# A two-layer decoder on one core: the order of the experts, the place of the excess code and of the scaling of x

## The chip, the cores and the metric

The kernel runs on one core of a Trainium2 chip. The metric is the device time of one execution in microseconds (us). A core has the engines TensorE (PE for its matmuls, PEld for its weight loads), VectorE (DVE), ScalarE (ACT) and GpSimd (POOL); SyncE (SP) issues nearly all DMAs here. "MB" below is one weight tile of 128 x 2048 fp32.

## The reference

Two decoder layers over 256 tokens of width 1024. In each layer three mixers (a convolution, differential attention, a gated linear recurrence) run on x and are merged, then `x = LN(alpha*x + mix)`; then a mixture of 32 experts, and `x = LN(alpha*x + moe)`. This is the part that the change touches:

```
g_idx = argmax(t @ wg + bg)                      # one of 4 groups per token
top_v, top_i = top_k(elog of that group, 2)      # two of its 8 experts
comb[token, expert] = softmax(top_v) * p_group
for e in range(32):
    h = silu(t @ w1[e]) * (t @ w3[e])            # w1, w3: 1024 x 512
    out = out + comb[:, e] * (h @ w2[e])         # w2: 512 x 1024
x = layer_norm(alpha * x + out)
```

An expert has 6 tiles of 1 MB (two each of w1, w3 and w2), all read from HBM in fp32. How many of the 512 token-expert pairs fall to an expert is known only when the kernel runs.

## The kernel before, in words

**Order of the experts.** Experts 0 to 3 are fixed. The other 28 are sorted on the chip by their number of tokens, rank 0 being the fullest (`sort`, L925), and `GROUPS` (L27) says in which order the ranks are worked: each tuple is four blocks of 32 token slots. Ranks 0 to 6 may use three blocks, 7 to 14 two, the rest one (`width`, L32). "Expert e" below is the e-th in this order: with the old order ranks 2, 3, 4, 5, 6 are experts 17, 19, 21, 23, 25 and ranks 27, 26, 25 are experts 22, 24, 26; experts 30 and 31 are the last group. Each block of an expert stands in an `If` on its count (`blocks`, L1282): a block without tokens is jumped over, and SP also jumps over the loads of an expert without tokens (L1414, L1415).

**Weights.** SP loads tiles into four rings of buffers, A to D, taken in the fixed order of `RING_ORDER` (8 B, 5 C, 5 A, 3 D: 21 tiles, L51). `room()` (L990) takes the next buffer, whether it is then filled or not, so an expert without tokens takes six buffers that stay empty. A load waits until the tile 21 places earlier has been used. At the end of iteration e the loads up to group e+3 are issued; a group is w1 and w3 of its expert and w2 of the one before.

**An iteration e** on PE: `between(e)` (L1346: the scatter of the last full group into the four output banks `po`, L1206 and L1207, then `turn_g(e-1)`, L1343, which transposes the hidden values of expert e-1), `hidden(e)` (L1305), `project(e-1)` (L1329), and for every eighth block the gather of the next token list (L1066, then L1081 to L1096). ACT and DVE split each projection in two fp32r halves (`split_y`, L1314 and L1316). In iteration 30 `between` also adds x to the banks (L1355), which needs x scaled.

**Three pieces near the end of the loop.** In iteration 25 `spilled()` (L1254) takes six buffers and jumps, on PE, DVE, ACT and SP, over code for experts that have more tokens than their blocks hold (`extra`, L1218; the trace has no instruction of it). In iteration 26 the last token list is gathered, and after the loads of that iteration `rows_of(0)` (L995) loads gain and bias of the norm into one buffer with two DMAs, and `affine` (L336) lets POOL compute `x = (x*g + b)*ALPHA` in twelve instructions (L340, L341, L343). x is raw before that; `gather` applies gain and bias to the gathered rows (`affine_g`, L1050).

**The next layer's small work.** `cw` (L506, the convolution's weights halved) and `ch` (L568, the gates' bias halved) are one DVE instruction each, behind a DMA (L505, L567). The kernel is scheduled by a planner that orders each engine's queue by its own simulated times, so such an instruction can stand in a queue far ahead of its place in the code.

The end of a layer (after the loop) projects expert 31 (L1440), adds it to the banks (L1446), and normalises (L1448 to L1466). L1440 comes behind `turn_g(31)`, and that behind `project(30)`.

Of the kernel before, what the change touches and what calls it, by code (L numbers as in the profile page):

```python
# [16 lines left out]
OP = mybir.AluOpType  # L17
# [6 lines left out]
STATIC = 4  # L24


GROUPS = [(8, 9), (10, 11), (12, 13), (0, 15), (14, 16, 17), (1, 18), (2, 19), (3, 20), (4, 27), (5, 26), (6, 25),  # L27
          (7, 21, 22), (23, 24)]
ORDER = [r for g in GROUPS for r in g]


# [9 lines left out]
NB = 4 * (len(GROUPS) + STATIC // 2)  # L41
NS = NB - 2 * STATIC
OWNER = [e for e in range(NE) for _ in range(width(e))]
ALPHA = (2 * DEPTH) ** 0.25
EPS = 1e-5
KC = 31
# [26 lines left out]
C_W, C_B, C_LG, C_LB, C_N = 0, 124, 128, 132, 136  # L73
G_B, G_LN, G_N = 0, 24, 56
# [94 lines left out]
def kernel(ctx: ExitStack, tc: tile.TileContext, *aps, layers=DEPTH, experts=NE, dbg=None):  # L169
# [3 lines left out]
    V, S, T, G = nc.vector, nc.scalar, nc.tensor, nc.gpsimd  # L173
# [24 lines left out]
    x = cp.tile([128, 2, 1024], F32, name="x")  # L198
# [137 lines left out]
    def affine(dst, g, b, eng, scale=1.0):  # L336

        for tb in range(2):
            for c in (slice(0, 512), slice(512, 1024)):
                eng.tensor_mul(dst[:, tb, c], x[:, tb, c], g[:, 0, c])  # L340
                eng.tensor_add(dst[:, tb, c], dst[:, tb, c], b[:, 0, c])  # L341
                if scale != 1.0:
                    eng.tensor_scalar(dst[:, tb, c], dst[:, tb, c], scale, None, op0=OP.mult)  # L343
# [5 lines left out]
    for l in range(layers):  # L349
# [4 lines left out]
        ch = lc.tile([128, G_N], F32, name="ch")  # L354
# [148 lines left out]

        cw = wk.tile([128, C_N], F32, name="cw")
        nc.sync.dma_start(cw, A["conv"][l])  # L505
        V.tensor_scalar(cw[:, C_W:C_W + 4 * KC], cw[:, C_W:C_W + 4 * KC], 0.5, None, op0=OP.mult)  # L506
        u = wk.tile([128, 4, 286], F32, name="u")
        G.memset(u[:, :, 0:30], 0.0)
        yc = wk.tile([128, 4, 256], F32, name="yc")
        pa2 = chunk_cm(1)  # L510
        begun = S.activation(yc, pa2, AF.Tanh, scale=0.5)
        pa1 = chunk_cm(0)
        V.scalar_tensor_tensor(u[:, :, 30:286], yc, 1.0, pa1, op0=OP.add, op1=OP.mult)

        with tc.high_priority(offset=-CONV_LOW):
            for pair in range(2):
# [48 lines left out]
            split(lth[:, tb, :], ltl[:, tb, :], pt)  # L565
        pq = chunk_cm(5)
        nc.sync.dma_start(ch, A["chan"][l])  # L567
        V.tensor_scalar(ch[:, G_B:G_B + 24], ch[:, G_B:G_B + 24], 0.5, None, op0=OP.mult)  # L568
        masks = wk.tile([128, 256], F32, name="masks")
        nc.sync.dma_start(masks, A["c_f"][:, F_UP + 128:F_UP + 384])  # L570
        ones, negm = masks[:, 0:128], masks[:, 128:256]
# [64 lines left out]
        for part in (1, 0):  # L636
            E = []
            for tb in range(2):
# [3 lines left out]
                for h in range(4):  # L642
# [8 lines left out]
                    for o, mv in pieces:  # L651
                        n = mv.shape[1]
# [342 lines left out]
        def rows_of(which):  # L995

            gb = room().rearrange("p (i d) -> p i d", i=2)
            for i in range(2):
                nc.sync.dma_start(gb[:, i, :], rowbc(A["lnp"][l, 2 * which + i], 1024))
            return gb  # L1000
# [49 lines left out]
        def affine_g(dst, src, k):  # L1050

            g, b = ch[:, G_LN + k:G_LN + k + 1], ch[:, G_LN + 8 + k:G_LN + 9 + k]
            if k % 2:
                return S.activation(dst, src, AF.Identity, bias=b, scale=g)
            return V.tensor_scalar(dst, src, g, b, op0=OP.mult, op1=OP.add)

        def gather(xg, gt, n):

            step = 512 // n
            for d0 in range(0, 8, step):  # L1060
                tag = ("gt", "h", "h", "y")[d0 // step % 4]
                pg = PB(tag, [128, step, n], 1 + (tag == "h"))
                for d in range(step):
                    c = slice(128 * (d0 + d), 128 * (d0 + d) + 128)
                    for tb in range(2):
                        mm = T.matmul(pg[:, d, :], x[:, tb, c], gt[:, tb, :], start=tb == 0, stop=tb == 1)  # L1066
                done = [affine_g(xg[:, d0 + d, :], pg[:, d, :], d0 + d) for d in range(step)]
            return [i.ins for i in (mm, *done[-2:])]

        def slots(gt, tb, n=256):  # L1070
# [147 lines left out]
        def extra(W, code_of, comb_of, base):  # L1218

            g1 = ew.tile([128, 2, 64], F32, name="gt4", bufs=1)  # L1220
            for tb in range(2):
                V.tensor_scalar(g1[:, tb, :], slot, float(base), code_of(tb), op0=OP.add, op1=OP.is_equal)

            def T2(shape):
                return ew.tile(shape, F32, name="ov", bufs=1)

            xo = T2([128, 8, 64])
            gather(xo, g1, 64)
            w = ew.tile([64, 1], F32, name="wso", bufs=1)
            pw = PB("gt", [64, 1], 1)  # L1230
            for tb in range(2):
                T.matmul(pw, g1[:, tb, :], comb_of(tb), start=tb == 0, stop=tb == 1)
            S.copy(w, pw)
            ps = PB("h", [128, 512], 2)
            mm_hidden(ps[0:64], ps[64:128], lambda k: xo[:, k, :], W, range(8))
            g = T2([64, 512])
            swiglu(g, ps[0:64], ps[64:128], w)
            gt = ew.tile([128, 4, 64], F32, name="sto", bufs=1)
            transpose_g(gt, g)
            ps = PB("y", [128, 512], 1)  # L1240
            pa, pb = ps[0:64, :], ps[64:128, :]
            mm_out(pa, pb, gt, W)
            pt = PB("gt", [64, 2, 128], 1)
            for tb in range(2):
                T.transpose(pt[:, tb, :], g1[:, tb, :], ident)
            st = ew.tile([64, 2, 128], F32, name="sto", bufs=1)
            S.copy(st, pt)
            for half, src in enumerate((pa, pb)):
                y = T2([64, 512])
                S.copy(y, src)  # L1250
                for tb in range(2):
                    T.matmul(po[half][tb], st[:, tb, :], y, start=False, stop=False)
# [108 lines left out]
        for e in range(experts):  # L1361
# [18 lines left out]
                scatter(sts[NB // 4 - 2])  # L1380

            b0 = 8 * len(lists_of)
            if b0 < NB and (OWNER[b0] == e + 2 or b0 == NB - 4 and e == experts - 6):
                n = min(8, NB - b0) // 4
                gt = ew.tile([128, 2, 256], F32, name="gt4", bufs=1)
                for tb in range(2):
                    slots(gt, tb, 128 * n)
                xg_next = ew.tile([128, 8, 256], F32, name="xg")
                with ExitStack() as after:
                    for ins in gather(xg_next[:, :, 0:128 * n], gt[:, :, 0:128 * n], 128 * n):  # L1390
                        after.enter_context(tc.issue_after(ins))
                    end = next((i for i in range(OWNER[b0], experts) if FIRST[i] >= b0 + 8), experts)
                    tokens(OWNER[b0], end - OWNER[b0])
                ws_next = ew.tile([128, 2, 4], F32, name="ws")
                weigh(ws_next, gt, lambda tb, i: comb_s[:, tb, b0 - 8 + 4 * i:b0 - 4 + 4 * i], n)
                lists_of[b0 // 8] = xg_next, ws_next
                st = turn(gt, n)
                for i in range(n):
                    sts[b0 // 4 + i] = st[:, i]
            if e == experts - 7:  # L1400

                spilled()

# [3 lines left out]
            for d in dict.fromkeys(p[0] for p in pieces):  # L1407
# [7 lines left out]
                with tc.If(sizes_sp[d] > 0, preferred_fallthrough_block=True):  # L1415
                    n = nc.values_load(who[0:1, d:d + 1], min_val=0, max_val=NE - 1, engines=[ENG.SP])
                    for w in ws_:
                        fetch(*w, n)
            if e == experts - 6:

                gb = rows_of(0)
                affine(x, gb[:, 0:1], gb[:, 1:2], G, ALPHA)
        if l == layers - 1:
            gb = rows_of(1)
        st = sm.tile([128, 2, 2, 6], F32, name="lnst")
# [66 lines left out]
```

## Time and profile before

| | us |
|---|---|
| median of 3 runs | 1570.54 |
| the runs | 1568.11, 1570.54, 1581.56 |
| the profiled execution, its time | 1580.48 |
| its span, first to last instruction | 1578.7 |
| PE busy | 1305.4 (83%) |
| DVE busy | 754.8 (48%) |
| ACT busy | 540.1 (34%) |
| POOL busy | 309.2 (20%) |
| mean granted TensorE clock | 0.939 |

The profiled execution is 9.9 us above the median, and 1.8 us of its time lie outside its span. The page also cuts the span in 40 slices: the DMA engines are full (9 tenths and over 400 GB/s) in slices 10 to 20 and 29 to 39, which are the experts of the two layers, and half empty while the mixers run. A row of the timeline gives start, duration, engine, line, operation and tiles, and in brackets how long the engine sat idle before it and what ended that.

### The profile page before, as it was taken

Reading aid. Unit: us, or ns where it says so; the run is one execution under the profiler, and the core shown is the slowest. Engines: PE = TensorE matmul, PEld = TensorE weight load, DVE = VectorE, ACT = ScalarE, POOL = GpSimd, SP = SyncE. Lnnn points to the kernel's source line nnn. Section 1 sums busy time; section 2 is a strip of 40 time slices with the busy share of each in tenths; the row PEclk is TensorE's granted clock in tenths of the full one; section 3 lists DMA queues with packets and bytes.
Section 4 is the critical chain, followed back from the end, with each engine's and each line's share of the span. In section 5 each row is a group of like instructions: output and inputs, shape, how many; then the busy total and the mean of one; then the engine's idle time right before and its main releaser. Section 6 shows DMA issues by size and latency. Waiting matters only on the chain. (4 is left out here: it accounts for less than half of the span.)

```text
span 1578.7 us, 32663 instructions
## 1 busy us (share of the span) xinstructions
PE 1305.4 (83%) x12222; PEld 966.4 (61%) x12222; DVE 754.8 (48%) x1721; ACT 540.1 (34%) x1200; POOL 309.2 (20%) x247
## 2 busy tenths in 40 slices
PE   8999999897886877765688999989888877787664
PEld 8878999764553544442287889987555545454332
DVE  4999876732222222121258998767432232322114
ACT  5744655322221222111246445553222221222111
POOL 5644432200000000001265553412000000000012
PEclk9999999899999999988889999999899999999688
DMA  9433448969999999989944334568799999997694
GB/s 352 158 113 114 144 138 348 360 268 417 418 418 416 417 412 417 413 362 417 379 145 157 128 108 147 174 242 345 290 405 417 414 417 417 414 402 306 263 369 165
DMA packets 72791, 481.66 MB, mean 305 GB/s; under 512 B 8576, under 2 KB 9600, under 8 KB 17152
## 3 DMA queue, kind: packets, MB, share of 16 engines
q1 hardware_dynamic: 72288, 478.27, 77.0%
q8 instruction: 135, 2.21, 0.6%
q14 instruction: 80, 0.66, 0.1%
q10 hardware_dynamic: 288, 0.52, 0.1%
HBM read 477.71 MB, written 1.05 MB: 303 GB/s over the span
## 5 line engine op out<-in xcount | busy, mean ns | idle before, releaser
L422 POOL TENSOR_TENSOR wlo<-wa,whi 128x512 fp32r<-128x512 f32 x187 | 253.7, 1365 | 317.2 <-ACT whi L421 309.9
L421 ACT CAST whi<-wa 128x512 fp32r<-128x512 f32 x312 | 190.9, 620 | 192.0 <-PE mm L429 102.4
L1316 DVE TENSOR_TENSOR yl<-y,yh 32x256 fp32r<-32x256 f32 (+1 forms) x252 | 104.8, 416 | 245.8 <-ACT yh L1314 160.8
L430 PE MATMUL mm<-xh,wlo 128*128 128x256 f32 x640 | 184.9, 289 | 8.5 <-DVE wlo L422 7.3
L428 PE MATMUL mm<-xh,whi 128*128 128x256 f32 x640 | 184.4, 288 | 5.4 <-ACT whi L421 5.3
L429 PE MATMUL mm<-xl,whi 128*128 128x256 f32 x640 | 183.9, 287 | 0.0
L1154 DVE SCALAR_TENSOR_TENSOR g<-g,h 64x256 f32<-64x256 f32 x73 | 30.2, 413 | 319.8 <-ACT g L1153 267.3
L340 POOL TENSOR_TENSOR x<-x,wa 128x512 f32<-128x512 f32 x8 | 9.9, 1274 | 825.6 <-DMA wa<-in_lnp_dram 825.6
L1305 PE MATMUL h<-wb,xg 128*32 128x256 f32 x1888 | 144.0, 414 | 27.1 <-DMA wb<-in_w_dram 18.2
L1314 ACT CAST yh<-y 32x256 fp32r<-32x256 f32 (+1 forms) x252 | 90.8, 360 | 194.3 <-PE y L1329 190.1
L1153 ACT ACTIVATE g<-h 64x256 f32<-64x256 f32 x73 | 27.5, 377 | 377.4 <-PE h L1305 377.4
L430 PEld LDWEIGHTS mm<-xh,wlo 128*128 128x128 f32 x640 | 124.4, 194 | 10.7 <-DVE wlo L422 8.3
L428 PEld LDWEIGHTS mm<-xh,whi 128*128 128x128 f32 x640 | 124.9, 195 | 5.8 <-ACT whi L421 5.6
L422 DVE TENSOR_TENSOR wlo<-wa,whi 128x512 fp32r<-128x512 f32 x125 | 98.8, 797 | 58.0 <-ACT whi L421 58.0
L429 PEld LDWEIGHTS mm<-xl,whi 128*128 128x128 f32 x640 | 124.8, 195 | 1.0 <-issue 0.3
L1305 PEld LDWEIGHTS h<-wb,xg 128*32 128x32 f32 x1888 | 71.6, 117 | 86.2 <-DMA wb<-in_w_dram 28.5
L526 DVE SCALAR_TENSOR_TENSOR pc<-u,cw,pc 128x256 f32<-128x256 f32 x232 | 112.9, 487 | 4.1
L1305 PE MATMUL h<-wa,xg 128*32 128x256 f32 x1136 | 96.2, 416 | 9.2 <-PEq L1284 3.4
L429 PE MATMUL mm<-wlo,xh 128*128 128x512 f32 x208 | 84.6, 407 | 3.7 <-DVE wlo L422 3.7
L428 PE MATMUL mm<-whi,xh 128*128 128x512 f32 x208 | 83.2, 401 | 1.6 <-ACT A L615 1.6
L430 PE MATMUL mm<-whi,xl 128*128 128x512 f32 x208 | 83.2, 400 | 0.0
L1305 PE MATMUL h<-wc,xg 128*32 128x256 f32 x912 | 75.5, 388 | 6.5 <-DMA wc<-in_w_dram 3.1
(411 smaller groups left out, 2356.7 us busy)
## 6 DMA issues: line engine op xcount, KB each, us to landing
wb<-in_w_dram SPq DMA_DIRECT2D x137, 1024.0 KB, 10.5
wc<-in_w_dram SPq DMA_DIRECT2D x87, 1024.0 KB, 10.1
wa<-in_w_dram SPq DMA_DIRECT2D x83, 1024.0 KB, 9.9
wd<-in_w_dram SPq DMA_DIRECT2D x47, 1024.0 KB, 10.7
wa<-in_w_cm_dram SPq DMA_DIRECT2D x39, 1024.0 KB, 5.0
wa<-in_w_tm_dram SPq DMA_DIRECT2D x20, 1024.0 KB, 5.0
wa<-in_w_br_dram SPq DMA_DIRECT2D x12, 1024.0 KB, 5.0
wa<-in_w_out_dram SPq DMA_DIRECT2D x8, 1024.0 KB, 5.6
```

The lines of the kernel that those rows point to most:

```text
L340: eng.tensor_mul(dst[:, tb, c], x[:, tb, c], g[:, 0, c])
L421: S.copy(hi, wv)
L422: (V if npiece[0] > 4 * l and npiece[0] % 4 < share[0] else G).tensor_sub(lo, wv, hi)
L428: T.matmul(ps, ah, bh, start=first, stop=False)
L429: T.matmul(ps, ah, bl, start=False, stop=False)
L430: T.matmul(ps, al, bh, start=False, stop=last)
L526: V.scalar_tensor_tensor(yc[:, b, :] if j == KC - 1 else acc[:, i, :], u[:, b, j:j + 256], wv, acc[:, i, :], op0=OP.mult, op1=OP.add)
L1153: S.activation(g[:, c], p1_[:, c], AF.Tanh, scale=0.5)
L1154: V.scalar_tensor_tensor(g[:, c], g[:, c], 1.0, p1_[:, c], op0=OP.add, op1=OP.mult)
L1305: T.matmul(ps[32 * q:32 * q + 32, :], xg[:, k, 32 * j:32 * j + 32], W[q // 2][k // 4][:, f:f + 256], start=k == 0, stop=k == 7)
L1314: S.copy(yh[o:o + n, c], p)
L1316: V.tensor_sub(yl[o:o + n, c], p, yh[o:o + n, c])
```

## The change

Four edits: another order of the groups (the ranks 25, 26, 27 go from experts 26, 24, 22 to 29, 25, 21; ranks 2, 3, 4 from 17, 19, 21 to 20, 22, 24; the group of one-block experts from 27 to 29 goes to 17 to 19); the last gather from iteration 26 to 27, `rows_of(0)` from the end of iteration 26 to 25 ahead of that iteration's loads, `affine` from 26 to 27; `spilled()` from 25 to 28, with its gather taking x already scaled (one DVE instruction instead of eight on DVE and ACT); and L506 and L568 made to issue after the DVE instruction that writes `u`, in their own layer.

```diff
-GROUPS = [(8, 9), (10, 11), (12, 13), (0, 15), (14, 16, 17), (1, 18), (2, 19), (3, 20), (4, 27), (5, 26), (6, 25),
-          (7, 21, 22), (23, 24)]
+GROUPS = [(8, 9), (10, 11), (12, 13), (0, 15), (14, 16, 17), (1, 18), (7, 21, 22), (2, 27), (3, 19), (4, 26), (5, 20),
+          (6, 25), (23, 24)]
...
-        V.tensor_scalar(cw[:, C_W:C_W + 4 * KC], cw[:, C_W:C_W + 4 * KC], 0.5, None, op0=OP.mult)
...
-        V.scalar_tensor_tensor(u[:, :, 30:286], yc, 1.0, pa1, op0=OP.add, op1=OP.mult)
+        gated = V.scalar_tensor_tensor(u[:, :, 30:286], yc, 1.0, pa1, op0=OP.add, op1=OP.mult)
+        with tc.issue_after(gated.ins):
+            V.tensor_scalar(cw[:, C_W:C_W + 4 * KC], cw[:, C_W:C_W + 4 * KC], 0.5, None, op0=OP.mult)
...
-        V.tensor_scalar(ch[:, G_B:G_B + 24], ch[:, G_B:G_B + 24], 0.5, None, op0=OP.mult)
+        with tc.issue_after(gated.ins):
+            V.tensor_scalar(ch[:, G_B:G_B + 24], ch[:, G_B:G_B + 24], 0.5, None, op0=OP.mult)
...
-        def gather(xg, gt, n):
+        def gather(xg, gt, n, scale=None):
...
+                if scale is not None:
+                    V.tensor_scalar(xg[:, d0:d0 + step, :], pg, scale, None, op0=OP.mult)
+                    continue
                 done = [affine_g(xg[:, d0 + d, :], pg[:, d, :], d0 + d) for d in range(step)]
+            if scale is not None:
+                return None
...
-            gather(xo, g1, 64)
+            gather(xo, g1, 64, 1.0 / ALPHA)
...
-            if b0 < NB and (OWNER[b0] == e + 2 or b0 == NB - 4 and e == experts - 6):
+            if b0 < NB and (OWNER[b0] == e + 2 or b0 == NB - 4 and e == experts - 5):
...
             if e == experts - 7:
+                gb = rows_of(0)
+            if e == experts - 5:
+
+                affine(x, gb[:, 0:1], gb[:, 1:2], G, ALPHA)
+            if e == experts - 4:

                 spilled()
...
-            if e == experts - 6:
-
-                gb = rows_of(0)
-                affine(x, gb[:, 0:1], gb[:, 1:2], G, ALPHA)
```

## Rows read from the trace of the kernel before

**Rows 1.** Windows: busy of PE, PEld, DVE, ACT, POOL; PEclk, DMA share, GB/s.

```profile
680.00:722.00 42.00, 24.93 (x248) 15.48 (x249) 6.81 (x19) 6.55 (x18) 0.00 (x0) 0.78 0.91 365
722.00:766.00 44.00, 30.70 (x339) 14.09 (x339) 8.36 (x20) 6.26 (x18) 12.18 (x10) 0.81 1.01 415
...
1400.00:1520.00 120.00, 90.40 (x957) 54.00 (x956) 25.97 (x63) 24.88 (x65) 4.77 (x4) 0.84 0.80 310
```

**Rows 2.** Timeline of SP, layer 1, the issues of weight tiles from 1388 us.

```profile
1388.34 9.64 SPq L1022 DMA_DIRECT2D wb<-in_w_dram  x4
1403.83 3.77 SPq L1022 DMA_DIRECT2D wc<-in_w_dram  x5
1407.94 0.33 SPq L1022 DMA_DIRECT2D wa<-in_w_dram  x1
1424.38 0.33 SPq L1022 DMA_DIRECT2D wd<-in_w_dram  x1
1425.11 8.35 SPq L1022 DMA_DIRECT2D wb<-in_w_dram  x5
1444.29 1.66 SPq L1022 DMA_DIRECT2D wc<-in_w_dram  x2
```

**Rows 3.** Waits of PE, longest first, in 1377:1521 and then in 1520:1550.

```profile
PE po L1206 <- DVEq L1284: 9.5, 1, 9.5
...
PE y L1329 <- DMA wb<-in_w_dram: 6.2, 2, 5.7
```

**Rows 4.** Timeline of PE, layer 1, where iterations of the loop begin or turn.

```profile
1368.64 3.66 PE L1305 MATMUL h<-wb,xg 128*32 128x256 f32 x64
...
1377.63 0.41 PE L1305 MATMUL h<-wb,xg 128*32 128x256 f32 x2
...
1403.55 4.64 PE L1305 MATMUL h<-wa,xg 128*32 128x256 f32 x64
...
1413.51 1.93 PE L1305 MATMUL h<-wd,xg 128*32 128x256 f32 x32
...
1431.95 1.05 PE L1343 MATMUL gt<-cf,g 128*128 128x128 f32 x4
...
1438.08 2.14 PE L1305 MATMUL h<-wc,xg 128*32 128x256 f32 x34
...
1462.71 5.77 PE L1305 MATMUL h<-wb,xg 128*32 128x256 f32 x64
...
1488.36 2.02 PE L1066 MATMUL gt<-gt,x 128*128 128x128 f32 x16 [0.64 <-ACT yh L1314]
...
1496.88 6.36 PE L1305 MATMUL h<-wa,xg 128*32 128x256 f32 x64
...
1506.77 3.66 PE L1305 MATMUL h<-wb,xg 128*32 128x256 f32 x64
...
1513.42 2.14 PE L1305 MATMUL h<-wc,xg 128*32 128x256 f32 x34
```

**Rows 5.** Line 1022 in 1369:1376: duration, first and last start; time to landing.

```profile
L1022 SPq DMA_DIRECT2D wa<-in_w_dram x4: 333/335/992, 1370.3 to 1374.0; - x4
...
DMA to landing us min/median/max: 9.8/10.8/13.5
```

**Rows 6.** Line 1260, the jump over the excess code, on PE: min/median/max ns.

```profile
L1260 PEldq COMPARE_BRANCH  x4: 71/3097/6397, 674.3 to 1471.5; - x4
```

**Rows 7.** Timelines of PE and, last, of POOL at the end of layer 1.

```profile
1547.98 1.06 PE L1305 MATMUL h<-wb,xg 128*32 128x256 f32 x12 [0.21 <-DMA wb<-in_w_dram]
...
1556.20 1.93 PE L1329 MATMUL y<-wb,gT 128*32 128x256 f32 x32
1560.18 1.08 PE L1440 MATMUL h<-wc,gT 128*32 128x128 f32 x32 [2.05 <-ACT gT L1344]
...
1542.75 5.86 POOL L343 TENSOR_SCALAR x<-x 128x512 f32<-128x512 f32 x4
```

**Rows 8.** Timeline of DVE in layer 0's last experts.

```profile
720.67 0.18 DVE L568 TENSOR_SCALAR ch<-ch 128x24 f32<-128x24 f32 x1 [11.41 <-DMA ch<-in_chan_dram]
```

## The prediction, made before the changed kernel was run

> **What bounds the kernel now.** I read the windows first. While the experts run, the DMA engines are the bound, with a share of 1.01 at about 415 GB/s, except in two stretches: 680 to 722 us in layer 0 (0.91) and 1400 to 1520 us in layer 1 (0.80) [rows 1]. The reader should see a full pipe with two dents. Against 1.01 they cost (1 - 0.91/1.01) x 42 = 4.2 us and (1 - 0.80/1.01) x 120 = 25 us. The second dent is the subject.
>
> SP's issues tell what makes it [rows 2]. A full pass of the rings is 8 wb, 5 wc, 5 wa, 3 wd. Here come 4 wb, 5 wc, then 1 wa, 1 wd, 5 wb, 2 wc, with pauses of 16.4 us (1407.94 to 1424.38) and 10.8 us (1433.46 to 1444.29). Counted along the ring the buffers left out are those of experts 22, 24 and 26: layer 1 has three experts without tokens, and as ranks are sorted they are ranks 27, 26 and 25. Each takes six empty buffers out of the 21, so SP may look ahead by 3.5 places, of which two are empty, and then waits for PE to get there.
>
> So PE's waits come next. From 1377 to 1521 us its longest is 9.5 us, and no weight is among the waits listed there; only from 1520 on does it wait for wb tiles again [rows 3]. PE, with the chain DVE and ACT make with it, is the bound of that stretch, and DMA stands still because PE is late with freeing buffers. From expert 19's first matmul at 1377.63 to expert 29's at 1513.42 [rows 4] it takes 135.8 us; eight of these experts have tokens, which at 2.5 us for each of six tiles is 120 us of DMA.
>
> At the end of each layer the page shows a tail. After expert 31's last hidden matmul (1547.98 + 1.06 = 1549.04) PE does project(30) only at 1556.20 and L1440 at 1560.18 [rows 7]: L1355 and the last scatter stand between. They stand there because POOL has x ready only at 1542.75 + 5.86 = 1548.61 [rows 7].
>
> **The groups, layer 1.** After the change the empty experts are 21, 25 and 29, and 17 to 19 have one block each. No 3.5 places hold more than one empty expert there, and `spilled`'s six buffers follow expert 30's. I add up PE's work from rows 4 by the nearest iterations, hidden start to hidden start.
> - Experts 20 and 24 (two blocks, one gather, one scatter) each like expert 19: 1403.55 - 1377.63 = 25.9; twice, 51.8.
> - The empty 21 and 25, each with project of a two-block expert: like 22, 1438.08 - 1431.95 = 6.1; twice, 12.2.
> - Expert 22 (two blocks, scatter, project(21) empty): 1431.95 - 1413.51 = 18.4, less a projection of 1.9: 16.5.
> - Expert 23: 1377.63 - 1368.64 = 9.0.
> - Expert 26 (one block, scatter, nothing to project): like 27, 1506.77 - 1496.88 = 9.9.
> - Expert 27 (one block and the half gather): 1513.42 - 1506.77 = 6.7, and 1496.88 - 1488.36 = 8.5: 15.2.
> - Experts 28 and 29 with the jump of `spilled`, a scatter and the empty place: like 25 and 26, 1488.36 - 1462.71 = 25.7, plus project(27), 1.9 + 0.8: 28.4.
>
> Sum 143.0 us to expert 30. The start is set by DMA, since 17 to 19 are now light: expert 20's four tiles are issued by 1374.0 and the slowest lands 13.5 us later [rows 5], at 1387.5; a block takes 3.7 us and its last quarter waits, so I put the start at 1385. Expert 30 then begins at 1528. To expert 31 come its block and turn (4.1), the empty project(29) (0.6), L1355 and the last scatter (5.3, between 1550.9 and 1556.2 in rows 7): 1538, and its hidden ends at 1541.7. Its tiles use the buffers of expert 29, free at about 1524; with the 9.8 us of the quickest landing in rows 5 and two more tiles of 2.5 us the last lands at 1539, while hidden(31) runs, so they hardly bind. The end of hidden(31) moves from 1549.0 to 1541.7, 7.3 us. Bounds: all 25 us of the dent, or nothing, if each row is dearer in its new place.
>
> **The scaling of x.** `rows_of` goes ahead of twelve weight tiles in SP's queue (groups 28 and 29); its 1 MB delays these by 2.5 us and is not loaded later, so nothing is lost. Its buffer is free again when POOL's twelve instructions are done, about 16 us after the gather of iteration 27; at rows 4's pace that is before iteration 30 asks for x, 28 us later. So L1355 and the scatter leave the tail. I expect project(30) 0.8 us after hidden(31) ends, as rows 4's iterations do, instead of 7.16 us (1549.04 to 1556.20): 6.4 us less, in both layers, as layer 0's tail has the same rows. In layer 0 it is a clear gain, since DMA bounds expert 31 there and the PE work fits in waits. In layer 1 too, since I have charged the 5.3 us above. The planner may keep the old place: then it is 0 in layer 0, and in layer 1 the 5.3 us only stay where they are. If x is late on POOL, PE waits in iteration 30, up to 16 us at worst.
>
> **`spilled` later.** The jump costs PE 6.4 us at worst [rows 6] and a wait of 9.5 with what hangs on it [rows 3]; it is in the sum above for layer 1. In layer 0 PE has slack at expert 28, as it waits for weights from there on. SP's own jump comes after the loads of group 30 and before those of 31: SP lets loads land first, which left most of the first dent's 4.2 us. It moves past twenty issues and I take it as unchanged, -1 to +4 us; I charge 1 us. The smaller body saves nothing in time unless run, and it isn't. The Trainium skill (Runtime: NRT & Kernel Launch, Instruction fetch mechanics) says that a taken branch whose target lies outside the fetched pages stalls until the page is fetched. By that a shorter body that is still too long makes the jump no cheaper, and the jumps over empty experts can cost the same as this one; rows 6 agree that such a branch takes anything from 0.07 to 6.4 us. By the rule alone, with three stalls of the longest kind added, the sum would come out like the first rival's.
>
> **The next layer's work.** L568 held DVE 11.41 us in layer 0 [rows 8], for a DMA that SP issued late between weights. But DMA ran on at 1.01 from 722 us [rows 1], and there the end of the layer hangs on DMA. So its removal is worth 0, at most the 1 us of the 4.2 that the jump does not explain. What was queued behind it, split_y and with it PE's scatter, is freed. In the new place the two instructions (0.2 us each) wait for `u`, with the convolution queued behind them on DVE: at most 0.4 us.
>
> **Sum.** Layer 0: -6.4 + 1 = -5.4. Layer 1: -7.3 - 6.4 = -13.7. Together -19.1, from 1580.48 to 1561.4 for the profiled execution. That one is 9.9 us above the median, and I take the same 19 us off the median: 1570.5 - 19.1 = 1551.4, say 1551.
>
> **The rivals.**
> - PE's chain is not shortened in layer 1. For: the work is the same, only its order differs, and the three jumps over empty experts and the one of `spilled` (rows 6: up to 6.4 us) fall where they fall. Against: three light experts now run while DMA bounds. With 2 us more on each of six jumps and turns, 12 us, layer 1 gains 2 instead of 14: 1570.5 - 5.4 - 2 = 1563.
> - The edits do not take hold: the planner keeps L1355 behind hidden(31), and empty buffers starve DMA in another place. Against: the rows of `rows_of` come twelve tiles, 30 us, earlier. About 1570.
> - Slower: expert 31's loads starve. Its six buffers were those of w2 of 27, of w1 and w3 of 29, and of w2 of 28, and six more before it stay empty, so SP can issue only when PE has passed iteration 29, which now lies behind the jump. In layer 0 I count PE there 25 us after expert 28's tiles land (5 for w2 of 27, 2.7 for its projection, 9.5 for the jump, 8 for scatter, turn and hidden(29)), and the loads should be issued from 30 us on (12 tiles at 2.5 us): a slack of 5 us. If PE is late by more, it decides. PE was 20 us late in layer 1 at such a place (expert 25, whose tiles were issued by 1433.5 [rows 2] and so landed near 1443, began at 1462.71 [rows 4]), and that would cost 15 us; with the tail not shortened and layer 1 dearer by 4 us, 1570.5 + 19 = 1589.
>
> **How the numbers follow.** The forecast has 0.57, with a range of its own of 1543 to 1558; the first rival 0.24, the second 0.11, the slower one 0.08. The range to hold the time 8 times in 10 goes from 1538 (another 13 us out of the dent) to 1569, past the first rival. A measurement of this kernel can tell about 1% from no change, 15.7 us. Faster by more than that, below 1554.8: most of the forecast and a few of the rest, 0.54. Within 1%: 0.37. Slower: 0.09.
>
> **What would show it.** Right: DMA share above 0.9 over expert 20 to 28 of layer 1; no DVE wait at L568; L1355 before hidden(31), and less than 2 us from hidden(31)'s end to project(30), in both layers; hidden(31) of layer 1 some 7 us earlier against the layer's start. Wrong: SP pauses of 10 us before expert 31's tiles; PE waiting for x in iteration 30; or L1355 still in the tail.

## The result, and the profile after

The changed kernel takes 1559.17 us (median of 9 runs, 1552.91 to 1561.87) against 1577.04 for the kernel before on the same chip: a ratio of 0.9884, with a 95% interval of 0.9865 to 0.9902. The forecast, 1551.4 off a median of 1570.5, is a ratio of 0.988. In microseconds the changed kernel lies 7.8 above the forecast and 1.2 above the forecast's own range (1543 to 1558), because six more runs of the kernel before moved its median up from 1570.54 to 1577.04; so the ratio is compared here, and the medians differ by 17.9 us, where the sum said 19.1. The profiled execution has a span of 1557.3 us against 1578.7, 21.4 less; the profiled execution of the kernel before lies 3.4 us above that kernel's median, which is most of the surplus.

By layers the sum also fits. Layer 1's first matmul of line 401 moves from 797.15 to 791.66 us, 5.5 earlier (forecast 5.4). Counted from there, layer 1's last projection starts (line 1440, now 1451) at 747.1 instead of 763.0, 15.9 earlier (forecast 13.7). Here are PE's first rows of line 401 in layer 1, before and after:

```profile
797.15 2.82 PE L401 MATMUL p<-cf,x 128*128 128x128 f32 x12 [8.97 <-DVE x L1459]
...
791.66 1.75 PE L401 MATMUL p<-cf,x 128*128 128x128 f32 x7 [8.97 <-DVE x L1470]
```

The windows show where the time went, with the columns and stretches of [rows 1]:

```profile
680.00:722.00 42.00, 29.34 (x349) 17.64 (x344) 9.34 (x23) 8.87 (x24) 15.73 (x12) 0.90 1.01 416
722.00:766.00 44.00, 29.48 (x268) 15.07 (x260) 6.84 (x16) 5.84 (x16) 0.00 (x0) 0.79 0.89 347
1400.00:1520.00 120.00, 96.64 (x999) 58.06 (x1001) 28.03 (x69) 27.21 (x70) 15.69 (x12) 0.87 0.93 372
```

Layer 1's dent is mostly filled: DMA share 0.93 instead of 0.80. In layer 0 the small dent has only moved, from 680:722 to 722:766. PE's timeline at the end of both layers answers to [rows 7] (line 1365 is x's entry into po, formerly 1355; 1315 is hidden, 1339 project, 1451 the last projection):

```profile
733.79 3.60 PE L1365 MATMUL po<-x,cf 128*128 128x512 f32 x8
...
768.06 3.48 PE L1315 MATMUL h<-wb,xg 128*32 128x256 f32 x28 [1.94 <-DMA wb<-in_w_dram]
772.27 1.93 PE L1339 MATMUL y<-wa,gT 128*32 128x256 f32 x32 [0.74 <-ACT gT L1354]
776.25 0.97 PE L1451 MATMUL h<-wc,gT 128*32 128x128 f32 x28 [1.68 <-ACT gT L1354]
...
1514.63 3.96 PE L1365 MATMUL po<-x,cf 128*128 128x512 f32 x8
...
1530.41 3.66 PE L1315 MATMUL h<-wb,xg 128*32 128x256 f32 x64
1534.82 1.93 PE L1339 MATMUL y<-wa,gT 128*32 128x256 f32 x32 [0.76 <-ACT gT L1354]
1538.80 1.08 PE L1451 MATMUL h<-wc,gT 128*32 128x128 f32 x32 [1.68 <-ACT gT L1354]
```

In both layers x enters po well before the last hidden, and project(30) follows that hidden by 0.74 and 0.76 us instead of 7.16. In layer 0 the last hidden still waits for weights and ends at 771.54, as before: only the tail went. The row before was

```profile
767.83 3.32 PE L1305 MATMUL h<-wb,xg 128*32 128x256 f32 x28 [1.50 <-DMA wb<-in_w_dram]
```

which ends at 771.15. In layer 1 it has no wait in brackets at all: PE was the bound, and its chain became shorter. PE's longest wait from 1377 to 1521 us, answering to [rows 3], is now a jump and no longer behind DVE:

```profile
PE po L1216 <- PEq L1294: 5.1, 1, 5.1
```

SP's issues in layer 1, answering to [rows 2], have lost the pauses of 16.4 and 10.8 us, but keep one of 12.3 us (1435.98 to 1448.29) and have a new one of 23.7 us:

```profile
1425.08 8.89 SPq L1024 DMA_DIRECT2D wb<-in_w_dram  x4
1434.37 1.61 SPq L1024 DMA_DIRECT2D wc<-in_w_dram  x3
1448.29 6.19 SPq L1024 DMA_DIRECT2D wa<-in_w_dram  x5
...
1484.82 1.98 SPq L1024 DMA_DIRECT2D wa<-in_w_dram  x4
1510.47 7.22 SPq L1024 DMA_DIRECT2D wb<-in_w_dram  x8
```

The issues at 1510.47, behind the long pause, are expert 31's. The prediction gave such a pause as a sign of failure; PE needed these tiles only at 1530.41, so it cost nothing there. So far the sizes and places of the sum are right. The experiments ask whether the parts did what the sum said they do.

### The profile page after: what moved, and what is told of

The parts are those of the page before. It is cut to its first block, busy times and chain, and to the rows that moved or that the text cites. A ratio compares the mean times of both kernels' runs of the same rounds, so it can differ in the third digit from the quotient of the medians.

```text
span 1557.3 us, 32665 instructions
## 1 busy us (share of the span) xinstructions
PE 1302.3 (84%) x12222; PEld 964.9 (62%) x12222; DVE 751.6 (48%) x1721; ACT 541.1 (35%) x1200; POOL 308.7 (20%) x247
## 5 line engine op out<-in xcount | busy, mean ns | idle before, releaser
L340 POOL TENSOR_TENSOR x<-x,wd 128x512 f32<-128x512 f32 x8 | 10.0, 1264 | 768.9 <-PE gt L1071 768.9
L430 PEld LDWEIGHTS mm<-xh,wlo 128*128 128x128 f32 x640 | 124.2, 194 | 11.1 <-DVE wlo L422 8.7
L1315 PEld LDWEIGHTS h<-wa,xg 128*32 128x32 f32 x1264 | 48.7, 113 | 50.5 <-issue 21.3
```

The source lines that it names most:

```text
L430: T.matmul(ps, al, bh, start=False, stop=last)
L1315: T.matmul(ps[32 * q:32 * q + 32, :], xg[:, k, 32 * j:32 * j + 32], W[q // 2][k // 4][:, f:f + 256], start=k == 0, stop=k == 7)
```

## The experiments

The parts are called groups (the order), scaling (`rows_of`, the last gather and `affine`), excess code (`spilled` at 28, its gather from scaled x) and tie (L506 and L568). First each one by itself in the kernel before, then each one taken out of the changed kernel, then places for the excess code.

**Groups alone.**

```diff
-... (2, 19), (3, 20), (4, 27), (5, 26), (6, 25), (7, 21, 22), (23, 24)]
+... (7, 21, 22), (2, 27), (3, 19), (4, 26), (5, 20), (6, 25), (23, 24)]
```

> Kernel before with the new order of the groups and nothing else. My theory: the three empty experts no longer take two places in 3.5 of SP's lookahead, so the dent of layer 1 shrinks from 25 us to under 12 us and hidden(31) of layer 1 ends 4 to 10 us earlier against the layer's start; both tails keep 7 us between hidden(31) and project(30). Time 4 to 10 us less, ratio 0.994 to 0.9975. Rival (the six buffers and the jump of spilled make the dent, not the order): dent stays over 18 us, time within 2 us of before.

Measured 0.9981 (0.9957 to 1.0004): nothing that can be told from no change. In the profile the last hidden of layer 1, counted from the layer's start, comes 6.0 us earlier, as the theory has it. But the windows row of this kernel shows a share of 0.85, which by the prediction's formula leaves 19 us of the dent, as the rival has it. It now lies in a pause at 1492 to 1505, behind the excess code's jump:

```profile
1400.00:1520.00 120.00, 91.02 (x967) 54.77 (x968) 29.68 (x72) 27.69 (x70) 9.79 (x9) 0.86 0.85 339
```

**Scaling alone.**

```diff
-            if b0 < NB and (OWNER[b0] == e + 2 or b0 == NB - 4 and e == experts - 6):
+            if b0 < NB and (OWNER[b0] == e + 2 or b0 == NB - 4 and e == experts - 5):
...
             if e == experts - 7:

                 spilled()
+                gb = rows_of(0)
+            if e == experts - 5:
+                affine(x, gb[:, 0:1], gb[:, 1:2], G, ALPHA)
...
-            if e == experts - 6:
-                gb = rows_of(0)
-                affine(x, gb[:, 0:1], gb[:, 1:2], G, ALPHA)
```

> Kernel before with only the scaling of x moved: rows_of in iteration 25, last gather and affine in iteration 27. My theory: L1355 and the last scatter leave both tails, project(30) follows hidden(31) by under 1 us instead of 7.2; 6 us less in each layer, 12 us in all, ratio 0.992, and the dent of layer 1 stays at 20 us or more. Rival (the tail is shortened only on paper, because the two pieces then delay hidden(31) by as much): under 4 us less.

Measured 1.0096 (1.0062 to 1.0129): slower, a miss on the wrong side. Three views of layer 0 of this kernel tell why. First SP's timeline:

```profile
742.53 0.34 SPq L567 DMA_DIRECT2D ch<-in_chan_dram  x1
763.14 3.77 SPq L194 DMA_DIRECT2D wa<-in_w_cm_dram  x4
767.80 9.79 SPq L1022 DMA_DIRECT2D wb<-in_w_dram  x8
778.54 4.22 SPq L1015 DMA_DIRECT2D wc<-in_w_dram  x4
```

Line 194 loads weights of the next layer's mixer. Here four of its tiles go ahead of the twelve pieces of expert 31; in the kernel before they came behind them:

```profile
770.51 4.82 SPq L194 DMA_DIRECT2D wa<-in_w_cm_dram  x5
```

Then DVE's timeline:

```profile
755.17 0.18 DVE L568 TENSOR_SCALAR ch<-ch 128x24 f32<-128x24 f32 x1 [42.71 <-DMA ch<-in_chan_dram]
```

DVE's wait of [rows 8] has grown from 11.41 to 42.71 us. And PE's timeline:

```profile
786.25 3.43 PE L1305 MATMUL h<-wb,xg 128*32 128x256 f32 x28 [1.48 <-DMA wb<-in_w_dram]
791.47 1.02 PE L1355 MATMUL po<-x,cf 128*128 128x512 f32 x2
...
794.12 1.02 PE L1355 MATMUL po<-x,cf 128*128 128x512 f32 x2
795.54 1.93 PE L1329 MATMUL y<-wb,gT 128*32 128x256 f32 x32
```

The last hidden ends at 789.68, 18.5 us late, and three quarters of L1355 still stand in the tail, although POOL had x ready some 70 us before (its last L343 ends at 719.03). So it is not POOL that keeps them there.

**Tie alone.**

```diff
+        with tc.issue_after(gated.ins):
+            V.tensor_scalar(cw[...], cw[...], 0.5, None, op0=OP.mult)
...
+        with tc.issue_after(gated.ins):
             V.tensor_scalar(ch[...], ch[...], 0.5, None, op0=OP.mult)
```

> Kernel before with only L506 and L568 tied to their layer. My theory: the wait of 11.4 us on DVE in layer 0 goes, and nothing else, since DMA bounds the end of that layer: within 2 us of before, ratio 0.999 to 1.001. Rival (that wait set back PE and so the weights): 5 to 10 us less, ratio 0.994 to 0.997.

Measured 0.9999 (0.9977 to 1.0021): nothing, as the prediction has it. In its profile the last hidden of layer 0 comes 3.5 us earlier (767.64), and layer 1's tail is 14.1 us instead of 11.1: the same matmuls took up to 1.9 us there instead of 1.0, at a granted clock of 0.73 against 1.00 in that stretch of the kernel before.

**Excess code alone.**

```diff
-            if e == experts - 7:
+            if e == experts - 4:
                 spilled()
...
-            gather(xo, g1, 64)
+            gather(xo, g1, 64, 1.0 / ALPHA)
```

with `gather` taking `scale` as in the change.

> Kernel before with only the excess code moved from iteration 25 to 28 (with its gather of scaled x). My theory: the dent loses the pauses at expert 28's tiles (6.8 us) but gets a pause of some 6 us before expert 31's, and PE keeps the jump: 0 to 5 us less. Rival (the six empty buffers beside those of experts 24 and 26 make the dent): dent under 12 us, 8 us or more less.

Measured 0.9955 (0.9931 to 0.9979), 7 us, more than the theory allowed. By itself this part makes both tails short (project 0.75 us after hidden) and brings layer 1's last hidden 11.1 us forward against the layer's start, more than the whole change did (9.5). But layer 0 lost. PE's timeline there:

```profile
736.07 0.80 PE L1212 MATMUL po<-yl,st 128*128 128x512 f32 x1 [28.07 <-DVE yl L1321]
...
777.65 3.66 PE L1310 MATMUL h<-wb,xg 128*32 128x256 f32 x64
782.06 1.93 PE L1334 MATMUL y<-wa,gT 128*32 128x256 f32 x32 [0.75 <-ACT gT L1349]
```

and DVE's:

```profile
734.04 1.07 DVE L568 TENSOR_SCALAR ch<-ch 128x24 f32<-128x24 f32 x1 [28.68 <-DMA ch<-in_chan_dram]
735.14 1.78 DVE L1321 TENSOR_TENSOR yl<-y,yh 32x256 fp32r<-32x256 f32 x4
```

DVE waits 28.68 us at L568 with an expert's yl queued behind it, PE waits for yl, and hidden(31) ends at 781.31, 10 us late. Alone the four parts come to -0.2, +1.0, 0 and -0.45%, a sum of +0.3%; together they are -1.16%. So what a part is worth depends on which others are there. The new theory: the excess code's new place and the tie carry the change; the first fixes the order of what comes after it, the second keeps a wait out that the first would make.

**The whole without the tie.**

```diff
-        with tc.issue_after(gated.ins):
-            V.tensor_scalar(cw[...], cw[...], 0.5, None, op0=OP.mult)
...
-        with tc.issue_after(gated.ins):
-            V.tensor_scalar(ch[...], ch[...], 0.5, None, op0=OP.mult)
+        V.tensor_scalar(cw[...], cw[...], 0.5, None, op0=OP.mult)
...
+        V.tensor_scalar(ch[...], ch[...], 0.5, None, op0=OP.mult)
```

> The whole change without its tie: L506 and L568 as before, groups, scaling and excess code as in the changed kernel. In the program order of VectorE the next layer's L568 then stands just ahead of an expert's yl, late in layer 0, and its load behind experts' weights in SP's queue. Theory (the tie keeps a wait out that the moved excess code and scaling would make): L568 waits 25 to 45 us for its load in layer 0 (11.4 in the kernel before, 28.7 and 42.7 in the two experiments that moved one part), PE stands idle behind yl, the last hidden of layer 0 ends 8 to 18 us later than in the changed kernel, ratio to before 0.994 to 1.000. Rival, as the prediction has it (the wait is off the path, the tie is worth 0): 0.987 to 0.990, as the changed kernel.

Measured 0.9966 (0.9949 to 0.9984), as the theory has it. DVE's timeline:

```profile
750.61 0.18 DVE L568 TENSOR_SCALAR ch<-ch 128x24 f32<-128x24 f32 x1 [37.45 <-DMA ch<-in_chan_dram]
750.82 1.78 DVE L1324 TENSOR_TENSOR yl<-y,yh 32x256 fp32r<-32x256 f32 x4
```

and PE's:

```profile
751.74 0.79 PE L1215 MATMUL po<-yl,st 128*128 128x512 f32 x1 [24.03 <-DVE yl L1324]
```

Layer 0's last hidden ends at 782.54, 11.0 us after the changed kernel's, and layer 1's experts take as long as there.

**Excess code and tie, without groups and scaling.**

Against the kernel before:

```diff
+        with tc.issue_after(gated.ins):
+            V.tensor_scalar(cw[...], cw[...], 0.5, None, op0=OP.mult)
...
-            if e == experts - 7:
+            if e == experts - 4:
                 spilled()
```

and, as in the two experiments with one part, the tie of L568 and the gather from scaled x.

> Kernel before with two parts of the change: the excess code at the fourth expert from the end with its scaled gather, and the tie. Groups and scaling of x as before. Theory (these two carry the change): the 10 us that the excess code alone lost in layer 0 come back, ratio 0.9955 less 0.005 to 0.009, that is 0.986 to 0.991. Rival (the groups or the moved scaling are needed for the gain): not under 0.993.

Measured 0.9927 (0.9906 to 0.9948): between the two. The wait at L568 is gone and hidden(31) of layer 0 ends at 773.11. x is now late: PE's timeline in layer 0 has

```profile
742.58 2.08 PE L1362 MATMUL po<-x,cf 128*128 128x512 f32 x2 [22.26 <-POOL x L343]
```

which is the "PE waits in iteration 30" of the prediction, above its 16 us. Most of it is covered: the tiles for expert 31's hidden had landed by 769.4, and PE began it at 769.45, without a wait. It ends 1.6 us after the changed kernel's.

**The whole with the old groups.**

```diff
-... (7, 21, 22), (2, 27), (3, 19), (4, 26), (5, 20), (6, 25), (23, 24)]
+... (2, 19), (3, 20), (4, 27), (5, 26), (6, 25), (7, 21, 22), (23, 24)]
```

> The changed kernel with the old order of the groups. Theory (excess code and tie carry the change, the order of the groups is worth nothing beside them): 0.986 to 0.991. Rival, as the prediction has it (the groups give a good part of layer 1's 13.7 us): 0.992 to 0.996.

Measured 0.9911 (0.9881 to 0.994), across both expectations. SP's two pauses of [rows 2] are back, and the windows row says 0.87:

```profile
1400.00:1520.00 120.00, 88.50 (x884) 52.33 (x886) 25.09 (x60) 24.07 (x61) 15.72 (x12) 0.84 0.87 346
```

So the groups do remove those pauses, but what this is worth in the whole is 0.0027 in ratio, and the intervals overlap. In the profile layer 1's experts take 429.4 us, 7.9 more than in the changed kernel, while layer 0's last hidden comes 4.9 us earlier.

**The whole with the excess code back at 25.**

```diff
             if e == experts - 7:
+                spilled()
                 gb = rows_of(0)
...
-            if e == experts - 4:
-                spilled()
...
-            gather(xo, g1, 64, 1.0 / ALPHA)
+            gather(xo, g1, 64)
```

> The changed kernel with the excess code back at the seventh expert from the end, gathering raw x as before. Theory (moving the excess code frees buffers and takes its jump out of the stretch where weights are short): layer 1's last hidden ends 3 to 6 us later than in the changed kernel and its last project 8 to 10, layer 0 as in the changed kernel within 3 us; 0.993 to 0.996. Rival (tie, groups and scaling carry it): 0.987 to 0.990.

Measured 1.0037 (1.0016 to 1.0058): slower than the kernel before, and far outside the theory, which asked too little. Layer 0 is 11.3 us late at its last hidden, which neither theory expected, and both tails are long again (9.8 us). SP's order is that of scaling alone: five tiles of line 194, then expert 31's twelve pieces. That left two explanations for the excess code's worth: its buffers and its jump, or the order that its place makes. The next runs tell them apart.

**The whole with the excess code at 29.**

```diff
-            if e == experts - 4:
+            if e == experts - 3:
                 spilled()
```

> The changed kernel with the excess code one expert later still, at the third from the end: expert 31's loads are issued before it, and x still goes into po right behind it. Theory (in the changed kernel the jump over the excess code holds SP ahead of expert 31's loads: 2.96 us of DMA lost in layer 0, 6.49 in layer 1, the place of the prediction's slower rival, and only layer 0 pays for it): both pauses go, the last hidden of layer 0 ends 2 to 3 us earlier, layer 1 within 2 us as PE binds there; 0.9855 to 0.988. Rival (the jump, now one expert nearer the end, has less waiting on PE to hide in and costs its 6 us in layer 0): 0.990 to 0.993.

Measured 0.9889 (0.9872 to 0.9906), the changed kernel's ratio. The pause ahead of expert 31's loads is gone: in 753:759 us the DMA share is 1.03 here and was 0.54 in the changed kernel. The row of this kernel's windows:

```profile
753.00:759.00 6.00, 3.44 (x37) 1.89 (x38) 2.58 (x6) 1.91 (x6) 0.00 (x0) 1.00 1.03 407
```

and that of the changed kernel's:

```profile
753.00:759.00 6.00, 3.76 (x23) 1.72 (x20) 1.69 (x4) 1.45 (x4) 0.00 (x0) 0.50 0.54 163
```

Layer 0's last hidden ends 6.2 us earlier (765.36), twice what was expected; the DMA time lost in the pause is 2.96 us of it, and the rest is not explained. So the pause is paid for in layer 0. But layer 1's experts take 4.9 us more, where at most 2 was expected. PE's timeline shows two waits there, at the jump over the excess code and for a weight tile:

```profile
1495.54 1.93 PE L1339 MATMUL y<-wb,gT 128*32 128x256 f32 x32 [2.31 <-DMA wa<-in_w_dram]
...
1515.25 5.10 PE L1365 MATMUL po<-x,cf 128*128 128x512 f32 x8 [7.55 <-issue]
```

In the changed kernel PE sat 4.00 us idle at its jump (ahead of 1510.20) and waited for no weight from 1480 to 1535. The two differences, 3.55 and 2.31 us, cover what layer 1 gives back; why the jump took 6.19 us here and 3.57 there is open.

**The whole with the old scaling.**

```diff
-            if b0 < NB and (OWNER[b0] == e + 2 or b0 == NB - 4 and e == experts - 5):
+            if b0 < NB and (OWNER[b0] == e + 2 or b0 == NB - 4 and e == experts - 6):
...
-            if e == experts - 7:
-                gb = rows_of(0)
-            if e == experts - 5:
-                affine(x, gb[:, 0:1], gb[:, 1:2], G, ALPHA)
...
+            if e == experts - 6:
+                gb = rows_of(0)
+                affine(x, gb[:, 0:1], gb[:, 1:2], G, ALPHA)
```

> The changed kernel with rows_of and affine back at the end of iteration 26 and the last gather in iteration 26: groups, excess code and tie as changed. Theory (the tail goes because the excess code's place in the program decides where x enters po): tail 4.7 us in both layers, PE waits some 20 us for x in layer 0 behind the excess code but the loads cover it; 0.987 to 0.991. Rival, as the prediction has it (the earlier scaling takes x's entry out of the tail, 6.4 us in each layer): tail 11 us, 0.996 to 0.998.

Measured 0.9898 (0.9882 to 0.9915), the theory's range and tail. PE's timeline of layer 0:

```profile
745.18 6.50 PE L1362 MATMUL po<-x,cf 128*128 128x512 f32 x8 [14.43 <-POOL x L343]
...
771.56 3.66 PE L1312 MATMUL h<-wb,xg 128*32 128x256 f32 x64
775.97 1.93 PE L1336 MATMUL y<-wa,gT 128*32 128x256 f32 x32 [0.75 <-ACT gT L1351]
```

PE waits 14.4 us for x, but L1362 stands before the last hidden and the tail is short, without the scaling having moved at all. The loads do not quite cover the wait, as the theory had it: expert 31's hidden begins without a wait, its tiles having landed by 765.5, and ends 3.7 us after the changed kernel's.

**The whole with the excess code at 13.**

```diff
+            if e == 13:
+                spilled()
...
-            if e == experts - 4:
-                spilled()
...
-            gather(xo, g1, 64, 1.0 / ALPHA)
+            gather(xo, g1, 64)
```

> The changed kernel with the excess code in iteration 13, gathering raw x, far from the stretch in question: its six buffers and its jump burden neither the dent nor expert 31. By buffers and jump alone this is as good as the changed kernel or better: 0.985 to 0.989, tail 4.7 us. Theory (what matters is that the excess code stands as a fence between x's entry into po and the next layer's first loads): without the fence x enters po in the tail as in the two experiments with it at 25 (tail 9.8 us) and the next layer's five w_cm tiles go ahead of expert 31's weights; the last hidden of layer 0 ends 10 to 15 us later; 0.998 to 1.004.

Measured 0.9999 (0.9987 to 1.0012). The place at 13 is best for buffers and jump, and layer 1's experts do take the least of all, 419.0 us. Yet the gain is gone. SP's timeline of layer 0:

```profile
745.25 0.34 SPq L568 DMA_DIRECT2D ch<-in_chan_dram  x1
747.77 6.20 SPq L194 DMA_DIRECT2D wa<-in_w_cm_dram  x5
755.16 15.41 SPq L1024 DMA_DIRECT2D wb<-in_w_dram  x8
771.52 4.22 SPq L1017 DMA_DIRECT2D wc<-in_w_dram  x4
```

and PE's:

```profile
780.50 1.06 PE L1315 MATMUL h<-wb,xg 128*32 128x256 f32 x12 [0.21 <-DMA wb<-in_w_dram]
783.34 1.02 PE L1365 MATMUL po<-x,cf 128*128 128x512 f32 x2
...
787.39 1.93 PE L1339 MATMUL y<-wb,gT 128*32 128x256 f32 x32
```

Five tiles of the next layer, 2.5 us of DMA each, go ahead of expert 31's; the last hidden ends at 781.56, 10.0 us after the changed kernel's. And x enters po in the tail again: 9.8 us in layer 0, 11.4 in layer 1. So both explanations hold, in different places. With the code at 25, 28 and 13 layer 1's experts take 430.9, 421.5 and 419.0 us: there the buffers or the jump count, not the order. At the end of layer 0 and in both tails the order on the queues counts, and here it costs about what layer 1 gains. No run put SP's order alone back; that the five tiles make the last hidden late is read from the timeline.

**A version from these.** The changed kernel with the excess code at 29 in layer 0 and at 13 in layer 1, and hidden(30) tied behind x's entry into po.

```diff
-            if e == experts - 4:
+            if e == (experts - 3 if l < layers - 1 else 13):
                 spilled()
...
-            gather(xo, g1, 64, 1.0 / ALPHA)
+            gather(xo, g1, 64, 1.0 / ALPHA if l < layers - 1 else None)
...
-                        T.matmul(po[half][tb], ident, x[...], start=False, stop=False)
+                        entered[0] = T.matmul(po[half][tb], ident, x[...], start=False, stop=False)
...
+                with nullcontext() if entered[0] is None else tc.issue_after(entered[0].ins):
-                hidden(e)
+                    hidden(e)
```

> A version made from what the runs so far showed: the changed kernel with the excess code at 29 in layer 0 (scaled x, its place before) and in iteration 13 in layer 1 (raw x), where no next layer's loads can go ahead of expert 31's; hidden(30) is tied behind x's entry into po, so that this can't fall into the tail. Theory: layer 0 as in the experiment with the excess code at 29 (last hidden near 765), layer 1's experts as in the one at 13 (419 to 421 us from the first hidden to the last, against 421.5 in the changed kernel and 426.4 with it at 29), tail 4.7 us: 1546 to 1552, ratio 0.981 to 0.985. Rival (layer 1's weights, loaded from layer 0's end on, arrive no earlier, so what layer 0 gains is waited for in layer 1): 0.987 to 0.990. Third way (the tie makes PE wait for x ahead of hidden(30), or the tail stays): 0.990 or more.

Measured 0.9866 (0.9833 to 0.9898). The tail is 4.7 us in both layers. In layer 1, with the code at 13, it was 11.4 without the tie, so the tie does explicitly what the excess code's place did by the way. Layer 0's last hidden is at 766.19. But layer 1's first hidden comes no earlier than in the changed kernel (1113.4 against 1112.6), and its experts take 422.9 us. The ratio lies between the theory's range and the rival's, with an interval over both, and can't be told from the changed kernel; the mechanism is the rival's, as the gain of layer 0 is gone by layer 1's first hidden.

The marks of the profiles, read off PE's timeline, in us. "Experts" goes from the first hidden of layer 1 to the end of its last, a tail from there to the start of the last projection.

| | last hidden, layer 0 | tail | layer 1 starts | its experts | tail | span | ratio |
|---|---|---|---|---|---|---|---|
| before | 771.2 | 11.1 | 797.2 | 433.8 | 11.1 | 1578.7 | 1 |
| changed | 771.5 | 4.7 | 791.7 | 421.5 | 4.7 | 1557.3 | 0.9884 |
| groups alone | 767.1 | 11.1 | 793.1 | 424.6 | 11.1 | 1569.3 | 0.9981 |
| scaling alone | 789.7 | 9.8 | 815.7 | 427.4 | 9.8 | 1589.8 | 1.0096 |
| tie alone | 767.6 | 11.1 | 794.5 | 432.5 | 14.1 | 1580.7 | 0.9999 |
| excess code alone | 781.3 | 4.7 | 801.7 | 423.2 | 4.7 | 1566.4 | 0.9955 |
| without tie | 782.5 | 4.7 | 802.7 | 421.1 | 4.7 | 1564.8 | 0.9966 |
| excess code and tie | 773.1 | 4.7 | 793.6 | 422.8 | 4.7 | 1563.4 | 0.9927 |
| old groups | 766.7 | 4.7 | 786.2 | 429.4 | 4.8 | 1564.9 | 0.9911 |
| excess code at 25 | 782.8 | 9.8 | 808.6 | 430.9 | 9.8 | 1586.6 | 1.0037 |
| excess code at 29 | 765.4 | 4.7 | 783.9 | 426.4 | 4.7 | 1554.6 | 0.9889 |
| old scaling | 775.2 | 4.7 | 795.5 | 420.2 | 4.7 | 1560.4 | 0.9898 |
| excess code at 13 | 781.6 | 9.8 | 807.1 | 419.0 | 11.4 | 1576.0 | 0.9999 |
| split version | 766.2 | 4.7 | 787.6 | 422.9 | 4.7 | 1559.5 | 0.9866 |

The tail is 4.7 us in every kernel whose excess code stands at 28 or 29, and 9.8 or more in every one where it doesn't, except in layer 1 of the split version, where the tie of hidden(30) holds it. These are single executions: layer 1's mixer, ahead of its first hidden, takes between 317.6 and 326.0 us in them, so differences of a few us between two spans say little.

## Why the prediction was right, and where its reasons were wrong

The total, both layers' shares and the signs at the tail and at the dent came out. That much of the sum rested on rows that were read rightly: the tail of 6.4 us, the dent, and PE as the bound of layer 1 but not of layer 0. The assignment of the terms to the edits was wrong in three places. The total did not suffer from it since the four edits were made together: that the edit which shortens the tail was among them, and the tie to keep out a wait which the prediction did not foresee, is luck. Taken out one at a time, the parts are worth 0.0276 in ratio together, over twice the 0.0116 of the whole, so none of them has a share of its own.

- **The scaling of x.** "So L1355 and the scatter leave the tail", 6.4 us in each layer, was put down to the scaling, because [rows 7] show POOL ready with x only at 1548.61. That late x was there, but it wasn't the cause. Scaling alone leaves the tail with x ready 70 us early; the old scaling in the whole leaves it out with x late. The excess code's new place takes L1355 out of the tail. The timelines show what it changed, the order on PE and SP, and the split version shows that this order on PE alone makes the tail short. That the planner counts the excess code's body as time spent, and so sees x ready by then, is a guess and wasn't tried. Beside that, moving the scaling is worth 0.0014 in ratio in the whole, within the noise; it takes a wait of 14.4 us for x away, of which layer 0's last hidden paid 3.7 in the one profile. The second rival's "the planner keeps L1355 behind hidden(31)" was the right fear, and the excess code's place was what decided it.
- **The excess code later** was charged 1 us. Taken back to 25, it costs 0.0153 in ratio, some 24 us, the largest part. By spans, against the changed kernel, the 29.3 us are 16.9 at the start of layer 1 (11.3 for expert 31's late weights, the longer tail for the rest), then 9.4 in layer 1's experts and 5.1 in its tail, less 2.1 in the mixer. The charge looked at SP's jump in layer 0 alone and missed that the move sets what stands behind it on SP and PE; what it does in layer 1's experts was counted under the groups.
- **The next layer's work**: "its removal is worth 0". In the kernel before this holds (0.9999). In the whole the tie is worth 0.0082, some 13 us, since without it L568 stands ahead of an expert's yl and waits 37.45 us instead of 11.41. The step priced the wait of [rows 8] as it was, not as it becomes when the work around it moves.

**The groups** had the right mechanism: [rows 2]'s pauses go with them and come back without them. With the old groups in the whole, layer 1's experts take 7.9 us more, near the 7.3 of the sum. But this too hangs on the other parts: with the excess code moved and the scaling not, they take 422.8 us with the old groups and 420.2 with the new ones. What the groups do in layer 0 is not settled: with the new ones its last hidden comes 4.1 us earlier in the kernel before and 4.9 us later in the whole, in single executions. In detail the chain of 143.0 us, from expert 20's start to expert 30's hidden, took 136.7: its data landed at 1383.79, so by the same rule it starts at 1381.2, it ends at 1521.85, and x's entry into po (4.0), which I had counted behind it, is left out. Single steps were off both ways, the two empty experts 8.5 us each instead of 6.1, the stretch of experts 28 and 29 with the jump 20.7 instead of 28.4.

**Slips in the working.** From expert 19's first matmul to expert 29's there are seven experts with tokens, eight only with 29 itself, so 105 us of DMA and not 120. Three stalls of 6.4 us would bring the forecast to about 1571, not to the first rival's 1563. And the rows of [rows 6] are not one branch of 0.07 to 6.4 us, as the last section shows.

**The rivals.** The first did not come, as layer 1's experts got 12.3 us shorter, nor the second, as L1365 left the tail. The third's place is real: SP stood still 13.1 us ahead of expert 31's loads in layer 0 (741.52 to 754.62) and 23.7 in layer 1, and by the run at 29 the one in layer 0 costs. It did not grow to a loss: layer 0's last hidden ends 0.4 us later than before, and layer 1's has no wait for weights.

## What to carry to other kernels

When a planner orders the instructions, an edit is worth what it does to the order on each engine's queue, not only its own cost: after a move, read on SP's queue what is loaded ahead of the weights that bound the stage, and on PE's what stands between the last wait and the end. Ask of a stall that is hidden now what will be queued behind it once its cover has moved. Parts that come to +0.3% one by one can be -1.16% together, so take each one out of the whole as well as trying it alone.

## What the hardware showed that was not expected

The jump over the excess code leaves two records on PE in each layer, a short and a long one. In the changed kernel, answering to [rows 6] (min/median/max in ns):

```profile
L1270 PEldq COMPARE_BRANCH  x4: 67/1822/6336, 720.6 to 1506.6; - x4
```

These are 71 and 6336 ns in layer 0 (at 720.6 and 723.0), 67 and 3572 ns in layer 1 (at 1505.4 and 1506.6). In the fourteen kernels the short record is 67 to 79 ns, and 21 of the 28 long ones lie between 6.0 and 6.4 us, the others between 3.4 and 7.4, with the excess code at 13, 25, 28 or 29, and with eight instructions in its gather or one. The Trainium skill (Runtime: NRT & Kernel Launch, Instruction fetch mechanics) says that a taken branch to a target outside the fetched pages stalls until that page is there; the long records agree with it. In layer 1 SP had no load under way at the jump, and from 1506.5 to 1510.3, which holds the long record, the core's DMA moved four packets, all on queues marked instruction:

```profile
q14 instruction: 3, 0.02, 2.1%
q8 instruction: 1, 0.02, 1.9%
```

The view does not say which engine they were for.

A wait of one DVE instruction of 0.18 us for a small DMA cost layer 0 about 11 us in the kernel without the tie (last hidden at 782.54 against 771.54): SP issued that DMA only at 738.00 us, between weights, and DVE had stood at it since 713.16.
